# Reciprocal of the pooling counts moved into the mixer, and the last split halves of form B22 issued without a tick between them

## The chip, the cores and the metric

One core of one Trainium2 chip. The metric is device microseconds (us) of one execution. Engines: PE is TensorE (matrix products), DVE VectorE, ACT ScalarE, POOL GpSimd, SP SyncE, which here only starts transfers. A transfer is a DMA; it can also be started from the queues of ACT and POOL.

## The reference, cut to what matters

One layer over 2048 positions of 1024 channels, all in float32:

```python
xn = rmsnorm(x, norm1_g)
u_pool, zq, zf, zi, zo, zg = split(xn @ w_in)
gates = sigmoid(zg + b_gate)                       # two sets of 1024
ya = pool_mixer(u_pool, pool_w, pool_scale) @ w_pa # trailing means over 2, 4, 8, 16 positions
yb = hgrn2_mixer(zq, zf, zi, zo, ...) @ w_pb       # gated linear recurrence, 4 heads
x = x + (gates[0] * ya + gates[1] * yb) @ w_o
x = x + conv_glu_ffn(rmsnorm(x, norm2_g), w_up, conv_w, conv_b, w_down)
out = rmsnorm(x, final_g)
```

In the pooling mixer a window's sum is divided by `minimum(t, w)`, with t the position counted from 1. So only the first 15 positions of the sequence need divisors other than the window's width w.

## The kernel before, in words

**Split products.** Each float32 matrix is split into a high half (rounded to the type fp32r, a copy on ACT, line 231 for weights and line 658 for inputs) and a low half (the rest, a subtraction on DVE, lines 232 and 659). A product is three matmuls: high by high, high by low, low by high. So PE can begin a product with the high halves, and needs the low half of an input or a weight one or two matmuls later. Names ending in `h` and `l` are the halves of an input; `ops` are the split weights (both halves in one tile).

**Seven products for eight.** Positions are worked in pairs of blocks of 512, and every weight matrix in 2x2 quarters. Instead of eight block products there are seven, P1 to P7, with combined inputs. Their input forms are B11, B21 and B22 (blocks) and T1 to T4 (sums and differences): P1 takes B11, P2 B21, P3 B22, P4 T4, P5 T1, P6 T2, P7 T3. `forms_a_task` makes B11 and B21 from the first 512 rows; `forms_b_task` makes T2, T1, T3, T4 and B22, in this order, from the second 512. Each form has four parts (k = 0 to 3), each of them split. In the traces, `x_T41l` is the low half of part 1 of T4 for the input projection, `m_B223h` the high half of part 3 of B22 for the feed-forward's up-projection. Forms whose name begins with x come from the layer's input, those with m from the mixer's result. Of the sequence's two pairs of blocks, each goes through the mixer and then the feed-forward; only the first pair prepares its x forms early (`early`).

**Banks.** PE sums into banks of PSUM, eight in all. Products share banks: P6, P7 and P4 add up in one called Z, P5 and P3 in V, P1 and P2 in X. Between P7 and P4 DVE reads Z and keeps the difference as `u3` (line 1316 in the projection of recurrence input and output gate, tiles `io_u`; line 1201 in `Unit`). P4 may not write Z before that.

**Order.** Work beside PE's is written as Python generators. `mm` (line 147) counts matmuls, and every sixth calls `tick`: the weight stream converts one operand more, and each task goes on to its next `yield`. `yield n` thus waits n ticks in program order. This sets in which order instructions are issued, and each engine then works through its queue in that order, waiting at the head for what the head needs. `behind(a, b)` keeps instruction a behind b on one engine without a wait between engines. A scheduler may still move an instruction by a few places. `Stream` converts weights ahead of use: `stream.room` is how many operands ahead, `stream.low` the last low half that it made.

**Around the change.** While the first pair's `proj_io` is at P7, `setup_task` (line 601) begins. It makes masks on POOL, and, after eight transfers that add weight quarters on POOL's queue (line 165, kept in `added`), `inv`: positions 1 to 16 (line 637), the minimum with each window (line 641, four instructions), and then their reciprocals on DVE (line 643, 128x64). `inv` is read by the pooling tasks (line 942). `mixer` calls `join(setup[0])` after `proj_io`, which finishes the setup if it isn't done. In the last loop of `forms_b_task` (from line 888) the four parts of B22 are split, with one tick after each (line 903); for the m forms this runs while PE is at P4 and P3 of the feed-forward's first two units (`up_0`, `up_1`). DVE's other work there: `h` (lines 1159 and 1160, results read from banks), `e` (lines 1613 and 1616, the convolution), and `ops` (line 232).

Of the kernel before, what the change touches and what calls it, by code (L numbers as in the profile page):

```python
# [81 lines left out]
def tile_trunk(  # L82
# [16 lines left out]
    pe, act, dve, pool, sp = nc.tensor, nc.scalar, nc.vector, nc.gpsimd, nc.sync  # L99
# [43 lines left out]
    def join(task):  # L143
        while task.live:
            task.step()
# [113 lines left out]
    def behind(ins, other):  # L259

        tc.add_manual_dep(ins.ins, other.ins.name, mybir.DependencyInfo(
            mybir.DependencyClass.NoSync, mybir.DependencyReason.DATA), reason="behind")
# [17 lines left out]
    stream = Stream()  # L280
# [232 lines left out]
    def prepare():  # L513
        todo = [sums[name].make(g) for name in ("wo", "up", "dn")
                for g in range(len(sums[name].groups))]
        active = []
        while todo or active:
            while todo and len(active) < 2:
                active.append(todo.pop(0))
            g = active.pop(0)  # L520
            try:
                lag = next(g)
            except StopIteration:
                continue
            active.append(g)
            yield lag
            while quiet[0]:
                yield 1
# [63 lines left out]
    inv = const.tile([P, 4, 16], F32, tag="inv", name="inv")  # L592
# [8 lines left out]
    def setup_task():  # L601
        scratch = [hist.rearrange("p a b -> p (a b)")[:, :64], uhist.rearrange("p a b -> p (a b)")]

        def mask_of():
            scratch.reverse()
            return scratch[0]

        keys = [(h, h, 0, h) for h in (1, 2, 4, 16)]
        keys += [(8 * h + t, 2 * h, t * h, h) for h in (4, 16) for t in range(2)]
        for key, x, off, w in keys:  # L610
            nb = 64 // x
            mf = mask_of()
            behind(pool.memset(mf, 1.0), last_root[0] if len(masks) < 6 else added[3])
            v = mf.rearrange("p (b h) -> p b h", h=x)
            pool.affine_select(out=v, in_=v, pattern=[[-2 * x, nb], [0, x]],
                               compare_op=ALU.is_ge, fill=0.0, base=-off, channel_multiplier=1)
            pool.affine_select(out=v, in_=v, pattern=[[2 * x, nb], [0, x]],
                               compare_op=ALU.is_ge, fill=0.0, base=off + w - 1,
                               channel_multiplier=-1)
            m8 = const.tile([P, 64], U8, tag=f"m{key}", name=f"m{key}")  # L620
            yield 2
            pool.tensor_copy(m8, mf)
            masks[key] = m8.rearrange("p (b h) -> p b h", h=x)
        for t in range(2):
            mf = mask_of()
            behind(pool.memset(mf, 0.0), added[3])
            pool.affine_select(out=mf, in_=mf, compare_op=ALU.not_equal, fill=1.0, base=-t,
                               pattern=[[-2, 64]], channel_multiplier=1)
            m8 = const.tile([P, 64], U8, tag=f"md{t}", name=f"md{t}")
            yield 2  # L630
            pool.tensor_copy(m8, mf)
            masks[-1 - t] = m8.unsqueeze(1)
        pool.memset(hist, 0.0)
        pool.memset(uhist, 0.0)
        while len(added) < 8:
            yield 1
        ins = pool.iota(inv[:, 3], pattern=[[1, 16]], base=1, channel_multiplier=0,
                        allow_small_or_imprecise_dtypes=True)
        behind(ins, added[7])
        for g, w in enumerate(WINDOWS):  # L640
            pool.tensor_scalar(inv[:, g], inv[:, 3], float(w), None, ALU.min)
        flat_inv = inv.rearrange("p a b -> p (a b)")
        dve.reciprocal(flat_inv, flat_inv)
        for h in range(HEADS):
            pool.memset(state[h, 0], 0.0)

# [5 lines left out]
    def split(src, name, on_pool=False):  # L652
        hi = slot(name + "h", TB, F32R)
        lo = slot(name + "l", TB, F32R)
        if on_pool:
            up = pool.tensor_scalar(hi, src, 1.0, 0.0, ALU.mult, ALU.add)
        else:
            up = act.copy(hi, src)
        low = dve.tensor_tensor(lo, src, f32(hi), ALU.subtract)
        last_split[0] = up, low  # L660
        return hi, lo
# [131 lines left out]
    def forms_b_task(src, gain, forms, full, after, go, early):  # L793
# [94 lines left out]
        while len(forms["B22"]) < 4:  # L888
            k = len(forms["B22"])
            while early and len(forms.get("gate", ())) < 4:  # L890
                yield 1
            forms["B22"].append(split(b22[k], f"{name}B22{k}"))
            if early:
                behind(last_split[0][1], forms["gate"][3])
                if k < 3:
                    stream.pins[25 + k] = last_split[0]
                    while len(stream.tiles) <= 25 + k:
                        if len(stream.tiles) - N_OPS >= stream.done:
                            yield 1
                        else:  # L900
                            stream.convert()
                stream.stop = 26 + k if k < 2 else None
            yield 1
        stream.room = LOOKAHEAD

    x2d = {}
# [1 line left out]
    def forms_of(kind, b, gain, after=lambda b: lambda j: None, early=False, go=lambda: True):  # L908
        forms = {k: [] for k in ("B11", "B21", "B22", "T1", "T2", "T3", "T4", "task")}
        full = {k: [] for k in ("B11", "B21", "T2")}  # L910
        first = Task(forms_a_task((kind, b), gain, forms, full, after(b), early))
        forms["task"].append(first)
        late = Task(forms_b_task((kind, b + 1), gain, forms, full, after(b + 1), go, early))
        return forms, first, late
# [371 lines left out]
    def proj_io(b0, forms, late, vd, zd):  # L1286
# [40 lines left out]
        for p in IO_ORDER:  # L1327
            if p == "P7" and not b0:
                setup.append(Task(setup_task()))
# [38 lines left out]
    def mixer(b0, forms, late):  # L1368
# [5 lines left out]
        proj_io(b0, forms, late, vd, zd)  # L1374
        if b0 == 0:
            join(setup[0])
            prep.append(Task(prepare()))


# [440 lines left out]
    for b in range(0, SEQ // TB, 2):  # L1820
        forms, task, late = nxt
        if b:
            join(task)
        forms, task, late = mixer(b, forms, late)
        join(task)
        nxt = ffn(b, forms, late)
# [50 lines left out]
```

## Time and profile before

| | |
|---|---|
| median of 3 runs | 2542.44 us (2541.99 to 2544.25) |
| the profiled execution | 2540.99 us |
| its span, first to last instruction | 2539.3 us |
| PE busy | 2511.9 us (99%) |
| DVE busy | 1979.2 us (78%) |
| ACT busy | 1176.5 us (46%) |
| mean granted clock of PE | 0.998 of full |

A row of a timeline gives the start in us, the duration, the engine (`q` behind its name: its queue), line, operation, output and inputs, the count of merged instructions, and in brackets how long the engine was idle before it and what ended that. `PEld` are the loads of the fixed operand, which overlap the matmuls. Buffer numbers are left out of the names, so the four `io_Z` banks have one name. A matmul's row lasts longer than the step to the next one, since matmuls overlap in the array.

### The profile page before, as it was taken

The numbers are of one execution on the slowest core, as the hardware profiler recorded it, in microseconds if no ns is written. First come the engines' busy times: TensorE is split into PE (matmuls) and PEld (weight loads), VectorE is DVE, ScalarE is ACT, GpSimd is POOL, SyncE is SP. The second block draws the span as 40 slices with busy tenths as digits, with TensorE's granted clock in tenths as the row PEclk, the third lists the DMA queues.
The fourth block names the chain that finished last, engine by engine and source line by source line (L and its number), as shares of the span: only waits on it lengthen the run. The fifth ranks groups of instructions, "written<-read, shape, count | busy, mean of one in ns | idle before, by whom it ended". The sixth has DMA issues, their size and how long they took to land.

```text
span 2539.3 us, 35647 instructions
## 1 busy us (share of the span) xinstructions
PE 2511.9 (99%) x11508; PEld 2054.1 (81%) x11508; DVE 1979.2 (78%) x3508; ACT 1176.5 (46%) x2218; POOL 752.6 (30%) x1127
## 2 busy tenths in 40 slices
PE   9999999999999999999999999999999999999998
PEld 7788887788788888888888888888887888888886
DVE  7799778498999777885586778765979888778755
ACT  6434434334545444554554343442355544445534
POOL 4334343002344334461230212200033432325410
PEclk9999999999999999999999999999999999999999
DMA  8787777767898889997444343447443454447952
GB/s 274 241 200 220 201 212 227 228 214 242 209 246 240 221 233 242 264 364 243 133 146 150 107 135 109 137 150 224 149 154 110 153 154 136 150 137 236 327 165 97
DMA packets 252331, 493.75 MB, mean 194 GB/s; under 512 B 26544, under 2 KB 43056, under 8 KB 251824
## 3 DMA queue, kind: packets, MB, share of 16 engines
q1 hardware_dynamic: 184512, 313.60, 39.1%
q0 software_dynamic: 42656, 112.74, 17.6%
q10 hardware_dynamic: 24976, 65.13, 7.5%
q8 instruction: 91, 1.49, 0.3%
q14 instruction: 96, 0.79, 0.1%
HBM read 381.79 MB, written 187.17 MB: 224 GB/s over the span
## 4 chain that ended last, share of the span: by engine, by line
PE 90%; DVE 6%; issue 1%; DMA 1%; ACT 1%; POOL 0%; SPq 0%; DVEq 0%; POOLq 0%; ACTq 0%
PE dn_P L148 16%; PE up_Z L148 14%; PE up_X L148 10%; PE up_V L148 9%; PE wo_P L148 6%; PE gr_Z L148 4%; PE pb L148 4%; PE pa L148 3%; PE gr_X L148 3%; PE gr_V L148 3%; PE fr_Z L148 2%; PE io_Z L148 2%; PE fr_X L148 2%; PE fr_V L148 2%; PE io_V L148 1%
## 5 line engine op out<-in xcount | busy, mean ns | idle before, releaser
L231 ACT CAST ops<-raw 128x512 fp32r<-128x512 f32 x744 | 459.7, 620 | 823.1 <-PE dn_P L148 180.5
L232 DVE TENSOR_TENSOR ops<-raw,ops 128x512 fp32r<-128x512 f32 x744 | 554.5, 749 | 218.3 <-ACT ops L231 210.3
L1613 DVE SCALAR_TENSOR_TENSOR e<-h,cols,e 128x512 f32<-128x512 f32 x176 | 143.6, 819 | 31.2 <-ACT e L1611 24.2
L1611 ACT ACTIVATE e<-h,cols 128x512 f32<-128x512 f32 x176 | 142.6, 814 | 25.6 <-DVE h L1160 18.9
L1616 DVE SCALAR_TENSOR_TENSOR e<-h,cols,e 128x512 f32<-128x512 f32 x176 | 134.0, 770 | 2.7
L962 POOL DMA_DIRECT2D g_P<-dg_P x154 | 84.0, 547 | 159.7 <-PE dn_P L148 113.3
L1270 POOL TENSOR_TENSOR gf_P<-e,e 128x512 f32<-128x512 f32 x44 | 62.2, 1415 | 149.6 <-DVE e L1622 93.0
L1270 POOL TENSOR_TENSOR gf_P<-gf_P,e 128x512 f32<-128x512 f32 x44 | 59.0, 1341 | 72.1 <-DVE e L1622 71.6
L1606 POOL COPY h<-h 128x2 f32<-128x2 f32 x88 | 40.9, 476 | 125.0 <-DVE h L1159 118.2
L1408 POOL TENSOR_TENSOR q<-q,qs 128x512 f32<-128x512 f32 x16 | 21.7, 1358 | 187.4 <-ACT qs L1407 180.8
L1445 ACT ACTIVATE gt<-gt,cols 128x512 f32<-128x512 f32 x48 | 34.8, 725 | 85.9 <-DVE gt L1160 61.3
L1620 ACT ACTIVATE e<-e 128x512 f32<-128x512 f32 x88 | 55.6, 631 | 39.8 <-DVE e L1616 39.4
L1608 POOL COPY hist<-h 128x2 f32<-128x2 f32 x88 | 37.8, 429 | 116.6 <-DVE h L1160 114.8
L1160 DVE TENSOR_TENSOR h<-up_u,up_V 128x512 f32<-128x512 f32 x88 | 60.1, 683 | 11.3 <-PE up_V L148 10.8
L1245 DVE TENSOR_TENSOR x<-x,wo_P 128x512 f32<-128x512 f32 x88 | 56.1, 683 | 12.0 <-PE wo_P L148 11.8
L1245 DVE TENSOR_TENSOR ac<-ac,dn_P 128x512 f32<-128x512 f32 x72 | 47.1, 682 | 16.8 <-PE dn_P L148 16.6
L1012 POOL COPY qm<-q 128x64 f32<-128x64 f32 x64 | 27.1, 452 | 99.0 <-issue 26.2
L1027 PE MATMUL pl<-qm,k 128*128 128x192 f32 x256 | 50.6, 327 | 3.7 <-DVE k L1048 3.6
L1636 POOL DMA_DIRECT2D dg_P<-gf_P x88 | 50.8, 577 | 8.3 <-POOL gf_P L1270 7.4
L1195 ACT COPY up_e<-up_X 128x512 f32<-128x512 f32 x44 | 25.8, 586 | 57.8 <-PE up_X L148 52.7
L1606 POOL COPY h<-hist 128x2 f32<-128x2 f32 x88 | 46.0, 530 | 20.6 <-issue 20.6
L1027 PEld LDWEIGHTS pl<-qm,k 128*128 128x128 f32 x256 | 43.9, 189 | 9.6 <-POOL u L926 2.3
(1285 smaller groups left out, 8088.4 us busy)
## 6 DMA issues: line engine op xcount, KB each, us to landing
g_P<-dg_P POOLq DMA_DIRECT2D x154, 256.0 KB, 6.0
raw<-in_w_up_t SPq DMA_DIRECT2D x132, 256.0 KB, 3.2
raw<-in_w_in_t SPq DMA_DIRECT2D x98, 256.0 KB, 3.3
dg_P<-gf_P POOLq DMA_DIRECT2D x88, 256.0 KB, 4.0
dg_P<-e SPq DMA_DIRECT2D x66, 256.0 KB, 3.8
raw<-in_w_dn SPq DMA_DIRECT2D x66, 256.0 KB, 3.7
x<-in_x SPq DMA_DIRECT2D x64, 256.0 KB, 4.9
gd<-gt ACTq DMA_DIRECT2D x64, 256.0 KB, 3.1
```

The costliest lines, as they stand in the source:

```text
L148: count[1] = pe.matmul(*args, **kw)
L231: self.mark = act.copy(hi, v)
L232: low = self.low = dve.tensor_tensor(lo, v, f32(hi), ALU.subtract)
L962: eng.dma_start(t, d)
L1027: ins = pe.matmul(pa_[:, c * 192 : c * 192 + 192], ks[:, (i + c) * P : (i + c + 1) * P], mv[:, c].rearrange("p s x -> p (s x)"), start=Tru ...
L1160: return dve.tensor_tensor(dst, t, ps, ALU.add if how == "add" else ALU.subtract)
L1245: dve.tensor_tensor(t, t, ps[j], ALU.add if sg > 0 else ALU.subtract)
L1270: pin(eng.tensor_tensor(t, x0, x1, op))
L1606: pool.tensor_copy(h[:, 0:2], hist[:, mt] if hf == 0 else hs[s, 0][:, TB : TB + 2])
L1611: in_turn(act.activation(t, h[:, 2:], AF.Identity, bias=col(o_cb + mt), scale=col(o_cw + 4 * MF + mt)))
L1613: in_turn(second(dve.scalar_tensor_tensor(t, h[:, 1 : 1 + TB], col(o_cw + 2 * MF + mt), t, ALU.mult, ALU.add)))
L1616: dve.scalar_tensor_tensor(t, h[:, 0:TB], col(o_cw + mt), t, ALU.mult, ALU.add)
```

## The change

The reciprocal leaves `setup_task` and is issued in `mixer` after the setup is joined, behind the stream's last low half. In the last loop of `forms_b_task` the tick after each part of B22 stays for the x forms and goes for the m forms, so that their four parts are issued in one go.

```diff
@@ setup_task
         for g, w in enumerate(WINDOWS):
             pool.tensor_scalar(inv[:, g], inv[:, 3], float(w), None, ALU.min)
-        flat_inv = inv.rearrange("p a b -> p (a b)")
-        dve.reciprocal(flat_inv, flat_inv)
         for h in range(HEADS):
             pool.memset(state[h, 0], 0.0)
@@ forms_b_task, last loop
                 stream.stop = 26 + k if k < 2 else None
-            yield 1
+            if src[0] != "m":
+                yield 1
         stream.room = LOOKAHEAD
@@ mixer
         if b0 == 0:
             join(setup[0])
+            flat_inv = inv.rearrange("p a b -> p (a b)")
+            behind(dve.reciprocal(flat_inv, flat_inv), stream.low)
             prep.append(Task(prepare()))
```

**The reciprocal on DVE.** In DVE's queue before, at P7 of the first `proj_io`, it stands between the first and the second of the four `io_u`:

```order
L865 TENSOR_TENSOR x_t_924<-x_b_364,x_t_563 128x512
L1316 TENSOR_TENSOR io_u_0_967<-io_Z_701,io_e_0_459 128x512
L643 RECIPROCAL inv<-inv 128x64
L1316 TENSOR_TENSOR io_u_1_977<-io_Z_702,io_e_1_469 128x512
L1316 TENSOR_TENSOR io_u_2_982<-io_Z_703,io_e_2_474 128x512
L1316 TENSOR_TENSOR io_u_3_987<-io_Z_704,io_e_3_479 128x512
L659 TENSOR_TENSOR x_T41l<-x_t_924,x_T41h 128x512
```

With the change it stands some 35 instructions further on, at the end of `proj_io`, behind a weight's low half for the first unit (`v` is a result of P3; the lines are those of the changed kernel):

```order
L1159 TENSOR_TENSOR v_1_3_1272<-io_u_3_779,io_V_788 128x512
L232 TENSOR_TENSOR ops_1253<-w31s_1250,ops_1253 128x512
L1377 RECIPROCAL inv<-inv 128x64
L232 TENSOR_TENSOR ops_1284<-raw_1018,ops_1284 128x512
L232 TENSOR_TENSOR ops_1307<-raw_1007,ops_1307 128x512
```

The four `io_u` now follow each other, and nothing else changes its place on DVE between the two positions.

**The low halves on DVE.** At P4 and P3 of the feed-forward's first units DVE's queue before was:

```order
L659 TENSOR_TENSOR m_B220l<-m_b_6612,m_B220h 128x512
L232 TENSOR_TENSOR ops_7028<-raw_6817,ops_7028 128x512
L659 TENSOR_TENSOR m_B221l<-m_b_6641,m_B221h 128x512
L1159 TENSOR_TENSOR h_0_1_0_6972<-up_0_Z,up_0_e_6548 128x512
L1613 SCALAR_TENSOR_TENSOR e_0_0_0_6975<-h_0_0_0_6716,cols,e_0_0_0_6975 128x512
L659 TENSOR_TENSOR m_B222l<-m_b_6676,m_B222h 128x512
L232 TENSOR_TENSOR ops_7043<-raw_6845,ops_7043 128x512
L1616 SCALAR_TENSOR_TENSOR e_0_0_0_6975<-h_0_0_0_6716,cols,e_0_0_0_6975 128x512
L659 TENSOR_TENSOR m_B223l<-m_b_6704,m_B223h 128x512
L1159 TENSOR_TENSOR h_1_1_0_7004<-up_1_Z,up_1_e_6568 128x512
```

and with the change it is:

```order
L657 TENSOR_TENSOR m_B220l<-m_b_6612,m_B220h 128x512
L232 TENSOR_TENSOR ops_7022<-raw_6817,ops_7022 128x512
L657 TENSOR_TENSOR m_B221l<-m_b_6641,m_B221h 128x512
L657 TENSOR_TENSOR m_B222l<-m_b_6676,m_B222h 128x512
L657 TENSOR_TENSOR m_B223l<-m_b_6704,m_B223h 128x512
L1158 TENSOR_TENSOR h_0_1_0_6985<-up_0_Z,up_0_e_6548 128x512
L1158 TENSOR_TENSOR h_1_1_0_7009<-up_1_Z,up_1_e_6568 128x512
L232 TENSOR_TENSOR ops_7043<-raw_6845,ops_7043 128x512
```

Part 2 has moved ahead of one `h` and one `e`, part 3 ahead of these, a weight and a second `e`. The same happens in the second pair's feed-forward.

**The high halves on ACT**, same place; before:

```order
L658 CAST m_B220h<-m_b_6612 128x512
L231 CAST ops_7028<-raw_6817 128x512
L658 CAST m_B221h<-m_b_6641 128x512
L1611 ACTIVATE e_0_0_0_6975<-h_0_0_0_6716,cols 128x512
L658 CAST m_B222h<-m_b_6676 128x512
L231 CAST ops_7043<-raw_6845 128x512
L307 DMA su3s_6097<-su3s_6096 16x16384
L658 CAST m_B223h<-m_b_6704 128x512
```

and with the change:

```order
L656 CAST m_B220h<-m_b_6612 128x512
L231 CAST ops_7022<-raw_6817 128x512
L656 CAST m_B221h<-m_b_6641 128x512
L656 CAST m_B222h<-m_b_6676 128x512
L656 CAST m_B223h<-m_b_6704 128x512
L231 CAST ops_7043<-raw_6845 128x512
```

Parts 2 and 3 now follow part 1 directly; the first `e` and the weight `ops_7043` come behind them. Further on, ACT's first Silu of `e` (line 1620, with the load of its table) has moved behind one weight and one `e` more.

## The prediction

> **What bounds the kernel now.** I read the page first, its busy shares and the chain that ended last, then the waits of PE, then the timelines around the longest of them.
>
> ```profile
> PE 2511.9 (99%) x11508; PEld 2054.1 (81%) x11508; DVE 1979.2 (78%) x3508; ACT 1176.5 (46%) x2218; POOL 752.6 (30%) x1127
> ...
> PE 90%; DVE 6%; issue 1%; DMA 1%; ACT 1%; POOL 0%; SPq 0%; DVEq 0%; POOLq 0%; ACTq 0%
> ```
>
> PE is busy for 99% of the span and is nine tenths of the chain, and the change takes no matmul away. So it can only win time in which PE stands still or runs slowly. The waits of PE (engine, line, releaser: us in total, times, longest) name two that the change touches:
>
> ```profile
> PE pl L1027 <- DVE k L1048: 3.6, 2, 1.9
> PE io_Z L148 <- DVE io_u L1316: 3.0, 1, 3.0
> ...
> PE up_V L148 <- DVE m_B223l L659: 1.8, 2, 0.9
> ```
>
> **First wait: io_Z for io_u.** The chain that ended last (start, us, what) shows what stands behind it:
>
> ```profile
> 70.88 3.84 DMA raw<-kw2ioP
> ...
> 75.28 0.35 POOL raw L165
> ...
> 78.28 0.26 POOL inv L641
> ...
> 78.56 0.04 DVE inv L643
> ...
> 79.71 12.26 PE io_Z L148 x45
> ```
>
> A weight's transfer lands, POOL can issue its addition, then POOL makes `inv`, then DVE inverts it, and only then comes the second `io_u`, for which PE waits. The pooling counts have nothing to do with `io_u`; the reciprocal merely stands ahead of it in DVE's queue. The timeline of this place:
>
> ```profile
> 74.64 0.69 DVE L1316 TENSOR_TENSOR io_u<-io_Z,io_e 128x512 f32<-128x512 f32 x1 [2.60 <-PE io_Z L148]
> ...
> 75.60 0.40 PE L148 MATMUL io_Z<-ops,x_T33l 128*128 128x512 f32 x1
> ...
> 75.84 0.63 PE L148 MATMUL io_Z<-ops,x_T40h 128*128 128x512 f32 x2
> 76.31 0.40 PE L148 MATMUL io_Z<-ops,x_T40l 128*128 128x512 f32 x1
> ...
> 78.56 0.55 DVE L643 RECIPROCAL inv<-inv 128x64 f32<-128x64 f32 x1 [3.23 <-POOL inv L641]
> 79.03 1.82 DVE L1316 TENSOR_TENSOR io_u<-io_Z,io_e 128x512 f32<-128x512 f32 x3
> ...
> 79.71 1.22 PE L148 MATMUL io_Z<-ops,x_T40h 128*128 128x512 f32 x2 [3.01 <-DVE io_u L1316]
> ...
> 80.77 0.68 DVE L659 TENSOR_TENSOR x_T41l<-x_t,x_T41h 128x512 fp32r<-128x512 f32 x1
> ...
> 81.97 0.68 DVE L232 TENSOR_TENSOR ops<-raw,ops 128x512 fp32r<-128x512 f32 x1
> ...
> 91.81 2.03 PE L148 MATMUL io_V<-ops,x_B220h 128*128 128x512 f32 x8
> ...
> 102.96 0.39 PE L148 MATMUL fr_X<-x_f0h,ops 128*128 128x512 f32 x1
> ```
>
> P4 and P3 of this stage are 48 matmuls each (4 parts, 4 banks, 3 products). P3 takes 102.96 - 91.81 = 11.15 us, 0.232 us a step. P4 takes 91.81 - 75.84 = 15.97 us. So this place loses 4.82 us, more than the 3.0 of the waits. A plain gap is 79.71 - (76.31 + 0.23) = 3.17 us; for the other 1.65 look at the windows, whose third number from the right is PE's granted clock:
>
> ```profile
> 76.50:79.70 3.20, 0.20 (x1) 0.00 (x0) 1.14 (x3) 0.00 (x0) 1.73 (x6) 1.00 0.91 136
> 79.70:83.50 3.80, 3.79 (x10) 3.06 (x11) 3.71 (x7) 1.14 (x2) 0.00 (x0) 0.55 0.16 28
> 83.50:91.80 8.30, 8.30 (x37) 6.74 (x36) 8.16 (x12) 7.65 (x14) 2.57 (x2) 1.00 0.77 233
> ```
>
> After the gap the clock is 0.55 for 3.8 us: 3.8 x 0.45 = 1.7 us, which is the rest.
>
> **Second wait: the low halves of B22**, once in each feed-forward:
>
> ```profile
> 682.97 0.40 PE L148 MATMUL up_V<-m_B223h,ops 128*128 128x512 f32 x1
> ...
> 684.24 0.50 PE L148 MATMUL up_V<-m_B223l,ops 128*128 128x512 f32 x1 [0.87 <-DVE m_B223l L659]
> 684.57 0.40 PE L148 MATMUL up_V<-m_B223h,ops 128*128 128x512 f32 x1
> ...
> 1933.97 0.39 PE L148 MATMUL up_V<-m_B223h,ops 128*128 128x512 f32 x1
> ...
> 1935.58 0.40 PE L148 MATMUL up_V<-m_B223h,ops 128*128 128x512 f32 x1
> ```
>
> Two steps of 0.23 take 684.57 - 682.97 = 1.60 us, so 1.14 us are lost; the second time 1.61, so 1.15. DVE and ACT at the first of the two:
>
> ```profile
> 679.77 0.69 DVE L659 TENSOR_TENSOR m_B221l<-m_b,m_B221h 128x512 fp32r<-128x512 f32 x1
> 680.37 0.69 DVE L1159 TENSOR_TENSOR h<-up_Z,up_e 128x512 f32<-128x512 f32 x1
> ...
> 683.50 0.69 DVE L659 TENSOR_TENSOR m_B223l<-m_b,m_B223h 128x512 fp32r<-128x512 f32 x1
> ...
> 679.18 0.81 ACT L1611 ACTIVATE e<-h,cols 128x512 f32<-128x512 f32 x1
> ```
>
> Between parts 1 and 3 DVE does an `h`, two `e`, a weight and part 2; an `e` stands between parts 1 and 2 on ACT.
>
> **The change part by part.**
>
> *Reciprocal away from P7.* DVE starts `x_T41l` and the low half of `ops` 1.20 us apart, with one more between, so 0.60 us is the step of a DVE instruction of 512. The second `io_u` starts at 74.64 + 0.60 = 75.24 instead of 79.03, the third at 75.84. The fourth waits for PE's last P7 matmul, 75.60 + 0.40 = 76.00, and ends at about 77.1. PE wants the second bank at 76.54, the third at 77.2, the fourth at 78.6: all three are in time, and 4.82 us go, the gap and the slow clock.
>
> What is late next? DVE goes on with `x_T41l` (77.05), a difference for T4 (77.65) and the low half of the next weight (78.25 to 78.95). In PE's queue, P4's seventeenth matmul is the first to read that low half, at 75.84 + 16 x 0.232 = 79.55. That is 0.6 us to spare, little, but enough. From there DVE is full up to P3:
>
> ```profile
> 88.98 1.79 DVE L659 TENSOR_TENSOR x_B220l<-x_b,x_B220h 128x512 fp32r<-128x512 f32 x1
> ...
> 93.67 1.10 PE L148 MATMUL io_V<-ops,x_B220l 128*128 128x512 f32 x4
> ```
>
> Before, this half ended at 90.77, 2.9 us before its use at 93.67. DVE comes 79.03 - 75.24 = 3.79 us earlier, PE 4.82, so 1.9 us remain. The transfers that fill P3's weights are issued by POOL as before, from 75.28 on, and the windows show DMA at 0.16 after 79.7: they have landed before ACT asks for them at about 82.
>
> *Reciprocal put back.* One instruction of 0.55 us in DVE's queue behind the last weight of `proj_io`, where its input is 20 us old. Its readers are the pooling tasks, the first of them at 181.5 (the count row of line 942; times are the shortest, middle and longest in ns, then first and last start in us):
>
> ```profile
> L942 DVE TENSOR_TENSOR p<-s,inv x4: 174/184/1011, 181.5 to 372.4; 128x16 f32<-128x16 f32 x4
> ```
>
> It costs DVE 0.55 us in a stretch in which DVE has over 9 us free, the first of these windows:
>
> ```profile
> 103.00:120.00 17.00, 17.00 (x75) 13.82 (x74) 7.68 (x12) 5.86 (x9) 3.58 (x3) 1.00 0.90 312
> 150.00:165.00 15.00, 13.09 (x63) 10.87 (x62) 14.43 (x45) 3.58 (x7) 6.23 (x9) 1.00 0.93 232
> ```
>
> The weight behind it is for P2 of the first unit, which PE begins four products of 12 matmuls, 11 us, after `fr_X` at 102.96: nothing lost. Without that cover it would cost 0.55.
>
> *B22 in one go.* Behind `m_B221l` (679.77), part 2 starts at 680.37 and part 3 at 680.97 and ends at 681.66, in place of 684.19. PE wants part 3 at 682.97 + 0.23 = 683.20: 1.5 us to spare. Their high halves follow at 679.18 and 679.7 on ACT, in the place of the first `e`, and are done by 680.3. So both stalls go: 1.14 + 1.15 = 2.29 us. What is put back are `h`, `e` and one weight, by 1.2 to 3 us. No matmul reads `h` or `e` before the down-projection. The weight `ops_7043` is read five products of 12 matmuls after P3 begins, 14 us later. The earlier return to four operands ahead changes only when ACT converts; I cost it at nothing.
>
> **Sum.** 4.82 + 2.29 = 7.11 us. The profiled execution has 2540.99 us (2539.3 span and 1.7 around it), so it would have 2533.9. It lies 1.45 below the median of the runs, 2542.44, which becomes **2535.3**, 0.28% less.
>
> **Rivals.**
>
> *The slow clock belongs to this one execution.* [...] As a mechanism of this kernel: if the timed runs mostly lack the stretch that the windows show, only 3.17 + 2.29 = 5.46 us go, and the median becomes 2537.0. For it: the gap is the only one over 2 us in PE's waits, so no second case shows that the clock always falls. Against it: the profiled execution has the stretch and is yet faster than all timed runs. Chance 0.12.
>
> *The recurrence takes it back.* In the stretch from 150 to 165 DVE is busy for 14.43 of 15 us, and there PE waits for `k` (line 1048), 1.9 us. If that chain does not start earlier, PE arrives 4.8 us sooner and waits that much longer: only B22's 2.29 remain, 2540.1. Against it: DVE's rows before, from 103 to 120, are mostly idle and wait for PE's results, so the chain starts with PE and moves along. Chance 0.14, with anything between the two.
>
> *It doesn't do what it says.* Another instruction takes the reciprocal's place, or ACT's high halves come late, and B22's stall stays: 2542.44 - 4.82 = 2537.6. Against it, every instruction between has a row above with time to spare. Chance 0.05.
>
> *Slower: the first Silu of each feed-forward.* ACT now has it and its table load behind one weight and one `e` more, and DVE's queue holds `up_u` of unit 3 behind a convolution that waits for ACT behind them. PE's P7 of that unit may not write the bank before:
>
> ```profile
> 693.51 0.68 DVE L1197 TENSOR_TENSOR up_u<-up_e,up_Z 128x512 f32<-128x512 f32 x1
> ...
> 701.46 0.40 PE L148 MATMUL up_Z<-m_T30h,ops 128*128 128x512 f32 x1
> ```
>
> There are 701.46 - 694.19 = 7.3 us to spare. What has moved ahead is one `e` (0.81 above) and one weight, which waits for PE's end of a product; with that wait I estimate 3 us. Were it 15, PE would lose 7.7 us twice, and the median would be 2542.44 - 7.11 + 15.4 = 2550.7; it is slower than before from 7.3 + 7.11/2 = 10.8 us on. Chance 0.03.
>
> **How the numbers follow.** The forecast has 0.66 and its own range is 2533.5 to 2537; the rivals have 0.12, 0.14, 0.05 and 0.03. 0.2% is 5.1 us, about what a measurement of this kernel can tell from no change; the line is at 2537.4. Faster by more: the forecast and half of the clock's rival, 0.72. Slower by more: the Silu, 0.03. Within: the rest, 0.25. The range goes from 2533.5, 1.8 below the forecast for waits that shrink with the shift, up to 2540.0, next to the recurrence's case.
>
> **What would show it.** Right: no wait of PE for `io_u`, P4 of the first projection in 11.2 us at clock 1.00; none for `m_B223l`; the pairs of `up_V` rows 0.46 us apart; the wait for `k` still about 1.9. Wrong: a new wait of PE for `ops` or `x_T41l` near 79, for `x_B22` parts near 88, or a longer one for `k` near 155.

## The result, and the profile after

The changed kernel takes **2533.76 us** (median of 6 runs, 2532.39 to 2536.34) against 2542.9 (6 runs, 2541.99 to 2544.25) beside it: ratio 0.9964, 95% interval 0.9951 to 0.9977, so 9.1 us less, with 5.8 to 12.5 in the interval. The forecast was 2535.3 and 7.1 us less. The profiled execution has 2532.39 us and a span of 2530.7, where the sum had 2533.9. Line numbers differ a little between kernels, since each has lines more or less; in the changed one `io_u` is 1315, the halves of inputs 656 and 657, the reciprocal 1377.

The page of the changed kernel, its busy shares and the shares of the chain that ended last:

```profile
PE 2509.1 (99%) x11508; PEld 2053.6 (81%) x11508; DVE 1978.5 (78%) x3508; ACT 1176.1 (46%) x2218; POOL 753.4 (30%) x1127
...
PE 91%; DVE 5%; issue 1%; DMA 1%; POOL 1%; ACT 1%; SPq 0%; DVEq 0%; POOLq 0%; ACTq 0%
```

PE is busy for 2.8 us less, with as many matmuls: those of the slow stretch count as busy and took longer (before, 8 in the 3.40 us from 79.70 on at clock 0.50, then 22 in 4.90 us at 1.00), and the stretch's 1.65 us are the larger part of it. Its waits (engine, line, releaser: us in total, times, longest):

```profile
PE x_t L722 <- DVE x_xs L716: 3.7, 5, 1.2
PE pl L1026 <- DVE k L1047: 3.5, 2, 1.8
PE pt L1144 <- DVE ot L1138: 1.8, 1, 1.8
PE warm L682 <- POOL ident L563: 1.4, 1, 1.4
PE ur_Z L148 <- DVE ur_u L1196: 1.1, 1, 1.1
```

Both waits that the change aimed at are gone, for `io_u` (3.0 before) and for `m_B223l` (1.8). Of the smaller ones a `gr_u` of 1.0 is missing too. The wait for `k` is as long as before. The windows of the first projection's P4 (length, busy time of PE, PEld, DVE, ACT and POOL, then PE's granted clock, DMA's share, GB/s), over the same times as before:

```profile
76.50:79.70 3.20, 3.20 (x16) 2.58 (x15) 3.11 (x6) 1.14 (x2) 2.46 (x4) 1.00 0.45 86
79.70:83.50 3.80, 3.80 (x18) 3.10 (x17) 3.66 (x7) 3.22 (x7) 1.82 (x4) 1.00 0.91 190
```

Where PE stood still for 3.00 of 3.20 us and then ran at clock 0.55 for 3.8, it now is busy throughout at 1.00. The timeline there:

```profile
74.52 2.48 DVE L1315 TENSOR_TENSOR io_u<-io_Z,io_e 128x512 f32<-128x512 f32 x4 [1.86 <-PE io_Z L148]
...
75.72 0.63 PE L148 MATMUL io_Z<-ops,x_T40h 128*128 128x512 f32 x2
...
78.13 0.68 DVE L232 TENSOR_TENSOR ops<-raw,ops 128x512 fp32r<-128x512 f32 x1
...
85.14 0.68 DVE L657 TENSOR_TENSOR x_B220l<-x_b,x_B220h 128x512 fp32r<-128x512 f32 x1
...
86.85 2.03 PE L148 MATMUL io_V<-ops,x_B220h 128*128 128x512 f32 x8
...
88.72 1.10 PE L148 MATMUL io_V<-ops,x_B220l 128*128 128x512 f32 x4
```

The four `io_u` run in one go, and P4 takes 86.85 - 75.72 = 11.13 us, where 11.2 was forecast and 15.97 measured before: 4.84 us. B22 in DVE's queue, and PE's steps beside it, in the first feed-forward:

```profile
673.49 0.69 DVE L657 TENSOR_TENSOR m_B221l<-m_b,m_B221h 128x512 fp32r<-128x512 f32 x1
674.09 0.69 DVE L657 TENSOR_TENSOR m_B222l<-m_b,m_B222h 128x512 fp32r<-128x512 f32 x1
674.70 0.68 DVE L657 TENSOR_TENSOR m_B223l<-m_b,m_B223h 128x512 fp32r<-128x512 f32 x1
...
676.66 0.39 PE L148 MATMUL up_V<-m_B223h,ops 128*128 128x512 f32 x1
676.89 0.40 PE L148 MATMUL up_V<-m_B223l,ops 128*128 128x512 f32 x1
677.13 0.39 PE L148 MATMUL up_V<-m_B223h,ops 128*128 128x512 f32 x1
```

The low half of part 3 ends at 675.38 and is wanted at 676.89, 1.5 us later, as forecast; the pair of `m_B223h` stands 0.47 us apart, where it was 1.60.

### The profile page after: what moved, and what is told of

It is laid out like the page before. It is cut to its first block, busy times and chain, and to the rows that moved or that the text cites. A ratio compares the mean times of both kernels' runs of the same rounds, so it can differ in the third digit from the quotient of the medians.

```text
span 2530.7 us, 35649 instructions
## 1 busy us (share of the span) xinstructions
PE 2509.1 (99%) x11508; PEld 2053.6 (81%) x11508; DVE 1978.5 (78%) x3508; ACT 1176.1 (46%) x2218; POOL 753.4 (30%) x1127
## 4 chain that ended last, share of the span: by engine, by line
PE 91%; DVE 5%; issue 1%; DMA 1%; POOL 1%; ACT 1%; SPq 0%; DVEq 0%; POOLq 0%; ACTq 0%
PE dn_P L148 16%; PE up_Z L148 14%; PE up_X L148 10%; PE up_V L148 10%; PE wo_P L148 6%; PE gr_Z L148 4%; PE pb L148 4%; PE pa L148 3%; PE io_Z L148 3%; PE gr_X L148 3%; PE fr_Z L148 2%; PE gr_V L148 2%; PE io_V L148 2%; PE fr_X L148 2%; PE fr_V L148 2%; PE pl L1026 1%
```

## The experiments

The theory is the sum of the prediction: DVE's wait for POOL's `inv` costs the gap and a slow clock behind it, and the ticks cost B22's two stalls. Against it stood that the slow clock was an accident of one execution, that the reciprocal's place or its own 0.55 us costs, and, since 2 us more came than the sum has, that one of the two parts carries something beyond its term.

### The reciprocal alone

```diff
@@ forms_b_task, against the change
-            if src[0] != "m":
-                yield 1
+            yield 1
```

> The reciprocal moved, the tick after each part of B22 kept. The change took 9.1 us off the median (2542.9 to 2533.76) where the prediction's sum was 7.1, so 2 us more have to be placed. Theory A (three pieces that add up, as predicted; the rest is small waits that shift): this kernel saves 4.8 us against before, 2538.1, and PE's two waits for m_B223l stay at 0.9 us each. Rival B (the 2 us more belong to the B22 part): also 4.8. Rival C (the gap ahead of io_u is longer in most executions than in the one profiled, since it ends when a weight's transfer has landed and POOL has made inv): 6 to 7 us, 2536.5.

Measured: 2537.36 us (11 runs, 2534.75 to 2540.16) against 2542.59 (21 runs): ratio 0.998, interval 0.9971 to 0.9989. That is 5.2 us for a term of 4.82. B22's two stalls are back in its waits of PE, beside longer ones for `gr_u`:

```profile
PE gr_Z L148 <- DVE gr_u L1195: 3.2, 2, 2.0
...
PE up_V L148 <- DVE m_B223l L657: 1.7, 2, 0.9
```

Every engine issues the same instructions in the same order as in the changed kernel until B22 is split, near 670 us. Yet ahead of that this profile is 3.5 us later than the changed kernel's. So the `gr_u` waits belong to the execution, not to the ticks.

### B22 alone

```diff
@@ forms_b_task, against the kernel before
-            yield 1
+            if src[0] != "m":
+                yield 1
```

> The ticks of B22 taken away, the reciprocal where it was before. Theory A: 2.3 us less than before, 2540.6; PE's waits for m_B223l are gone, the wait for io_u is there with a slow clock behind it. Rival B: 4 us or more less. Rival C: 2.3 us, and a wait for io_u that differs from the 3.0 us of before's trace, since its end depends on when the transfer lands. If the slow clock belongs to one execution alone, the clock after the gap is 1.00 here.

Measured: 2540.09 us (11 runs, 2536.71 to 2542.83) against 2542.59: ratio 0.999, interval 0.9981 to 0.9999. That is 2.5 us for a term of 2.29, and no wait for `m_B223l`. The two parts alone make 5.2 + 2.5 = 7.7 us. In its trace the gap for `io_u` is there again and longer than in the profile of before, and again a slow stretch follows. Its windows:

```profile
76.60:80.30 3.70, 0.10 (x1) 0.00 (x0) 1.12 (x3) 0.00 (x0) 2.25 (x7) 1.00 0.73 104
80.30:81.20 0.90, 0.87 (x3) 0.73 (x4) 0.90 (x2) 0.00 (x0) 0.00 (x0) 0.89 0.83 148
81.20:84.50 3.30, 3.30 (x9) 2.58 (x8) 3.22 (x6) 1.14 (x2) 0.00 (x0) 0.51 0.12 9
```

PE resumes at 80.33, has a few steps of the usual length, and is then at clock 0.51 for 3.3 us, in which every matmul takes 0.43 us instead of 0.23.

### The reciprocal behind the second, and behind the third io_u

The diff is that of the first of the two kernels; the other has `u3s[2]`.

```diff
@@ setup_task, against the change; u3s collects the io_u of the stage
+        flat_inv = inv.rearrange("p a b -> p (a b)")
+        behind(dve.reciprocal(flat_inv, flat_inv), u3s[1])
@@ mixer
-            flat_inv = inv.rearrange("p a b -> p (a b)")
-            behind(dve.reciprocal(flat_inv, flat_inv), stream.low)
```

> The changed kernel, with the reciprocal behind the second io_u. PE has three matmuls more before it must wait, so the gap is 3 x 0.23 = 0.7 us shorter than with the reciprocal behind the first: about 2.5 us if inv is ready at 78.5. If every gap of this kind is followed by a slow stretch, the clock is about 0.55 for some 4 us after it and P4 takes 11.15 + 2.5 + 1.7 = 15.3 us. If the clock falls only after about 3 us of standing still, it stays 1.00 and P4 takes 13.6 us.

> The changed kernel, with the reciprocal behind the third io_u. PE has three matmuls more of P4's first part and three of its second before it must wait: a gap of about 1.1 us if inv is ready at 78.5, more if it is late. By a threshold of about 3 us the clock stays 1.00 and P4 takes 12.3 us; if every gap brings the slow stretch, 14 us.

Measured, one run each: 2541.72 us behind the second, 2538.55 behind the third. DVE's wait does not shrink, since POOL is no earlier: the reciprocals start at 80.67 and 80.06, after idle times of 3.94 and 3.06 us. The expectations had `inv` ready at 78.5, and so their gaps of 2.5 and 1.1 us are missed: P4 takes 16.60 us instead of 15.3, and 14.22 instead of 12.3. What changes is how many banks PE can fill in the meantime. Windows of the two kernels, the second one and then the third:

```profile
78.10:81.80 3.70, 0.10 (x1) 0.00 (x0) 1.13 (x3) 0.00 (x0) 2.24 (x7) 1.00 0.75 112
81.80:83.10 1.30, 1.28 (x5) 1.05 (x6) 1.30 (x3) 0.00 (x0) 0.00 (x0) 0.98 0.46 82
83.10:86.50 3.40, 3.40 (x9) 2.67 (x8) 3.17 (x6) 2.01 (x4) 0.00 (x0) 0.50 0.30 78
```

```profile
79.20:81.20 2.00, 0.07 (x1) 0.00 (x0) 1.15 (x3) 0.00 (x0) 0.68 (x3) 1.00 1.01 163
81.20:83.00 1.80, 1.20 (x4) 0.67 (x4) 1.75 (x3) 0.62 (x2) 0.00 (x0) 1.00 0.33 57
```

Behind the second, a gap of 3.7 us and again a stretch of 3.4 us at half clock; so this kernel did not try a gap under 3 us, as it was meant to. Behind the third, a gap of 2.0 us and clock 1.00 behind it. The threshold of about 3 us in the two expectations was the author's supposition: no run shows it, and elsewhere the clock fell behind waits of 1.8 and 2.0 us too (last section). In the kernel with the reciprocal behind the third P4 also meets the wait that the prediction named as next in line, the low half of the weight behind the late `io_u`; the timeline of that kernel:

```profile
81.21 0.74 PE L148 MATMUL io_Z<-ops,x_T40h 128*128 128x512 f32 x2 [1.94 <-DVE io_u L1319]
...
83.01 0.50 PE L148 MATMUL io_Z<-ops,x_T41h 128*128 128x512 f32 x1 [0.60 <-DVE ops L232]
```

### One tick fewer, and twice the ticks

```diff
@@ forms_b_task, against the change: the first kernel
-            if src[0] != "m":
+            if src[0] != "m" or k < 2:
                 yield 1
@@ the second kernel
-            if src[0] != "m":
-                yield 1
+            yield 2 if src[0] == "m" else 1
```

> The change, but of the ticks of the m forms only those after part 2 and part 3 go; the one after part 0 and the one after part 1 stay. In DVE's queue one h, two e and one weight then stand among parts 2 and 3 again, as before. If only the place in DVE's queue matters: the two stalls for m_B223l are back, 0.9 us each in the waits and 1.1 us each in the steps, no wait for io_u, and a time 2.3 us over that of the change, about 2536. If it is the number of ticks that matters: half of the stalls, 2535. The first 670 us issue the same instructions in the same order as the change on every engine, so what differs there in the small waits (gr_u, k, at) is the difference between two executions; I expect up to 3 us in all.

Measured in one run: 2537.19 us, and `m_B223l` has its two waits of 0.9 again. Among the four parts there is one tick fewer than in the kernel before, yet DVE's queue holds the same there, two others between parts 1 and 2 and two between parts 2 and 3. The number of ticks does not decide; what stands in DVE's queue among the parts does.

> The change with two ticks after each part of the m forms where the kernel before has one. Part 3 then stands ten places behind part 0 in DVE's queue, against eight before and four in the change. If DVE's place sets the stall: at 0.62 us a place part 2 comes 2.4 us late and part 3 hardly later than that, so PE loses about 2.4 us in each feed-forward against 1.14 before and 0 in the change: 4.8 us over the change, about 2538.6. If DVE has slack that catches up: no more than the stall of before, 2536.

Measured: 2539.12 us (11 runs, 2536.76 to 2542.06), ratio 0.9985, interval 0.9976 to 0.9994, against 2533.04 of the change on the same chip: 6.1 us given back, 4.8 expected. Its timeline, DVE's rows and then PE's:

```profile
676.29 0.68 DVE L657 TENSOR_TENSOR m_B221l<-m_b,m_B221h 128x512 fp32r<-128x512 f32 x1
676.89 0.68 DVE L1157 TENSOR_TENSOR h<-up_Z,up_e 128x512 f32<-128x512 f32 x1
677.50 0.74 DVE L1616 SCALAR_TENSOR_TENSOR e<-h,cols,e 128x512 f32<-128x512 f32 x1
678.16 0.68 DVE L232 TENSOR_TENSOR ops<-raw,ops 128x512 fp32r<-128x512 f32 x1
678.76 0.74 DVE L1613 SCALAR_TENSOR_TENSOR e<-h,cols,e 128x512 f32<-128x512 f32 x1
679.42 0.68 DVE L657 TENSOR_TENSOR m_B222l<-m_b,m_B222h 128x512 fp32r<-128x512 f32 x1
...
678.24 0.50 PE L148 MATMUL up_V<-m_B222h,ops 128*128 128x512 f32 x1 [0.48 <-ACT m_B222h L656]
680.16 0.50 PE L148 MATMUL up_V<-m_B222l,ops 128*128 128x512 f32 x1 [1.42 <-DVE m_B222l L657]
680.49 0.39 PE L148 MATMUL up_V<-m_B222h,ops 128*128 128x512 f32 x1
```

DVE is not idle for a moment here; four instructions between parts 1 and 2 make the low half of part 2 late. PE waits first for its high half, from ACT (0.48 us), and then for the low half (1.42 us), which ends the stall. By the starts of the matmuls, set against those of the change, PE loses 2.50 us here and 2.49 in the second feed-forward, where the places in DVE's queue gave 2.4. Part 3's low half follows part 2's directly and costs nothing more.

### The reciprocal in its old place, its input earlier

```diff
@@ setup_task, against the change
-        while len(added) < 8:
+        while len(added) < 6:
             yield 1
...
-        behind(ins, added[7])
+        behind(ins, added[5])
...
+        while len(added) < 8:
+            yield 1
+        flat_inv = inv.rearrange("p a b -> p (a b)")
+        while not u3s:
+            yield 1
+        behind(dve.reciprocal(flat_inv, flat_inv), u3s[0])
@@ mixer
-            flat_inv = inv.rearrange("p a b -> p (a b)")
-            behind(dve.reciprocal(flat_inv, flat_inv), stream.low)
```

> The change with the reciprocal back in its old place, between the first and the second io_u in DVE's queue; instead POOL makes its input two weight transfers earlier, behind the sixth and not the eighth. If the loss was DVE's wait for POOL: the input is ready near 73 us, the reciprocal costs 0.6 us of DVE, the second io_u ends at about 76.5 against 76.54, the low half of the weight at 79.5 against 79.5, so nothing over 0.3 us is lost, and the time is that of the change, 9 us under the kernel before. If the reciprocal's place itself costs: a wait of PE for io_u or ops of 1 us or more at 76 to 80, and 2 us or more of the gain gone.

Measured: **2533.6 us** (5 runs, 2531.43 to 2535.81) against 2542.97 (15 runs): ratio 0.9965, interval 0.9952 to 0.9977, the same as the change. Its timeline:

```profile
71.15 2.11 POOL L643 TENSOR_SCALAR inv<-inv 128x16 f32<-128x16 f32 x4
...
74.69 0.69 DVE L1323 TENSOR_TENSOR io_u<-io_Z,io_e 128x512 f32<-128x512 f32 x1 [1.85 <-PE io_Z L148]
...
75.30 0.54 DVE L649 RECIPROCAL inv<-inv 128x64 f32<-128x64 f32 x1
...
75.75 1.82 DVE L1323 TENSOR_TENSOR io_u<-io_Z,io_e 128x512 f32<-128x512 f32 x3
...
76.59 0.62 PE L148 MATMUL io_Z<-ops,x_T40h 128*128 128x512 f32 x2
```

With its input ready at 73.26 the reciprocal starts as soon as DVE is free, between the first and the second `io_u` as before, and PE has no gap: the second bank's matmul stands where it should, 0.24 us behind the first bank's last. So neither the reciprocal's place nor its 0.54 us cost anything; its wait for POOL did, and moving POOL's five instructions for `inv` up by two weight transfers is worth as much as moving the reciprocal.

### The change once more

> The changed kernel once more, as it is, on the chip that runs the other kernels of this call. 9 us under the kernel before. If the 1.5 to 2 us beyond the named terms belong to the change, its profile has the small waits of the first one (gr_u 0.4, k 3.5, at none). If they belong to single executions, gr_u, k and at differ by 1 to 3 us again, as they do between the change and the reciprocal alone, which issue the same up to 670 us.

Measured: 2533.04 us (5 runs, 2532.01 to 2539.77) against 2542.97: ratio 0.9966, interval 0.9953 to 0.9978. Its waits of PE have a `gr_u` that the first profile of the change lacks, and less of `k`:

```profile
PE pl L1026 <- DVE k L1047: 1.5, 1, 1.5
PE pl L1026 <- POOL u L925: 1.5, 1, 1.5
...
PE gr_Z L148 <- DVE gr_u L1196: 1.3, 2, 1.1
```

## Why the prediction was right, and what its size missed

**The reciprocal's wait, 4.82 us.** Right in mechanism and size. P4 went from 15.97 to 11.13 us; by the starts of the same matmuls in both traces 4.85 us are gained between 72 and 100 us. That the wait and not the instruction costs was argued in the prediction and is shown by the kernel with the earlier input.

**What is late next.** Right: nothing. The low half of the weight ends at 78.81 and is read at 79.45, 0.6 us to spare as forecast; the kernel with the reciprocal behind the third `io_u` delays it and PE waits 0.60 us for it. `x_B220l` has 88.72 - 85.82 = 2.9 us to spare, 1.0 more than forecast, because its row is 0.68 us long and not 1.79. The step that put POOL's transfers "as before, from 75.28 on" failed: in the change POOL issues them at 77.15, and `inv` is ready only at 81.73, 3.2 us later than before. No weight came late, and with the reciprocal gone from there nothing waits for `inv`; it is inverted at 99.9 and first read at 176.3.

**B22, 1.14 + 1.15 us.** Right in mechanism: both waits gone, and with the order of before they return in each kernel that has it. By the starts of the matmuls the two places gave 1.17 and 1.21 us.

**The slow clock as an accident (chance 0.12).** Wrong as put: of three traces with a gap over 3 us (3.17, 3.79 and 3.79 between the end of a step and the next matmul) all three have the slow stretch, and it cost 8 matmuls x 0.2 us, about 1.6, each time. But a part of it stands: behind the same wait of 1.8 us the clock fell in one execution and not in another (last section), and that moves single executions.

**The recurrence takes it back (0.14).** It did not. The wait for `k` at 154.02 is 1.77 us against 1.9, and DVE's chain came forward with PE, as the row against this rival had it.

**Slower by the first Silu (0.03).** It did not come about. Rows of the changed kernel, `up_u` of unit 3 and the matmul that needs its bank:

```profile
686.80 0.68 DVE L1196 TENSOR_TENSOR up_u<-up_e,up_Z 128x512 f32<-128x512 f32 x1
...
694.02 0.40 PE L148 MATMUL up_Z<-m_T30h,ops 128*128 128x512 f32 x1
```

6.5 us to spare of 7.3; what moved ahead of it cost 0.7 us (before, it ended at 694.19, which is 686.7 in times of the changed kernel), where 3 were estimated.

**The size.** 9.1 us came where the sum had 7.1; in the two later comparisons 9.9 (the change again) and 9.4 (the earlier input). That 2533.76 lies in the forecast's own range, 2533.5 to 2537, is in part luck: the same kernel run again took 2533.04. The term that is short is B22's; the rest can't be given to the change by these runs. This table has the start of the same matmul in each kernel's trace less that in the first trace of the change, in us, at times of the latter:

```
                        72     100    660    700    1260   1300   1900   1940   end
before                  0.12   4.97   6.28   7.45   7.25   6.44   6.95   8.16   8.57
B22 alone               0.12   5.60   8.18   8.20   8.20   7.62   7.60   7.60   7.60
reciprocal alone        0.44   0.44   3.51   4.66   4.47   3.99   4.48   5.73   6.16
one tick fewer          0.04   0.04   2.17   3.33   3.14   2.66   3.14   4.35   4.77
earlier input           0.17   0.18   1.09   1.12   1.12   1.17   1.14   1.14   1.14
the change once more    0.21   0.21   0.90   0.93   0.93   0.97   0.95   0.95   0.95
```

Three things are to be read from it. *B22:* from 660 to 1260 and from 1300 to the end the three kernels with the old order lose 3.1 us (before: 0.97 + 2.13; reciprocal alone: 0.96 + 2.17; one tick fewer: 0.97 + 2.10), the three others, with the new order, nothing. The stalls are 2.4 of it (660 to 700, and 1900 to 1940). Another 0.7 is the sum of differences of under 0.03 us in single steps of the matmuls, 0.2 less from 700 to 1260 and 0.9 more behind 1300, the same in all three; the prediction's "I cost it at nothing" for what moves around B22 missed them, and what makes them stays open. *The gap:* 5.5 us in the trace of B22 alone against 4.85 in that of before, since POOL was later. *The rest:* between 1260 and 1300 the first four kernels gain 0.5 to 0.8 us on the change, at the second pair's transpositions, where PE waits 0.8 us for `x_xs` in the trace of the change and 0.3 in that of before; neither term has this, and its cause stays open. And between 100 and 660 these kernels differ by up to 3.1 us, though the reciprocal alone, one tick fewer and the change once more issue the same there as the change itself, instruction by instruction; the two that differ most of these, the reciprocal alone and one tick fewer, have a slow stretch there (at 390 and 467). So 4.8 to 5.5 and 3.1, together 7.9 to 8.6 us, are the change's by mechanism; the half to 2 us beyond, and the 0.5 to 0.8 that the transpositions may take back, are within the scatter of such small waits and within the interval, and these runs can't resolve them.

## What to carry to other kernels

Before a wait of the busiest engine is priced, look at what its releaser itself waits for: here an instruction of 0.55 us that nobody needed for another 100 us stood at the head of a queue and held three others, and either moving it or feeding it earlier brought the same. In an engine's queue without idle time count the places between the parts of an operand: here each was worth 0.6 us, and the ticks put four of them between parts 1 and 3, 2.4 us against a slack of 1.5. And where a trace shows slow matmuls behind a gap, price them with the gap: 1.65 us beside 3.17 here.

## What the runs showed of the hardware

**PE's clock behind a wait.** In six places windows of these traces show a lower granted clock behind a wait of PE, 0.50 to 0.58. In the trace of before it is 0.50 from 79.70 to 83.10, directly behind the gap, and 1.00 from there on; in those of B22 alone and of the reciprocal behind the second `io_u` it falls 0.7 and 1.2 us after PE resumed, an estimate from the clocks of 0.89 and 0.98 in the windows above. The waits ahead of the six were 3.0 us for `io_u` (before), 3.6 for `io_u` (B22 alone, and behind the second `io_u`), 2.0 for `gr_u` (the reciprocal alone) and 1.8 for `ot` (B22 alone, and one tick fewer).

Behind other waits of 1.8 to 1.94 us the clock stayed at 1.00: 1.9 us for `k` and 1.8 for `ot` in the trace of before, 1.94 for `io_u` behind the third, 1.8 for `ot` in the change once more. All ten traces have the wait of 1.8 us for `ot` (line 1138 in the change). Windows there, of the kernel with one tick fewer and of the change once more:

```profile
464.90:466.90 2.00, 0.36 (x2) 0.00 (x0) 1.41 (x3) 1.66 (x3) 0.00 (x0) 1.00 1.06 274
466.90:470.40 3.50, 3.30 (x9) 2.61 (x10) 2.71 (x7) 0.00 (x0) 0.00 (x0) 0.57 1.11 269
470.40:474.00 3.60, 3.60 (x17) 2.92 (x17) 0.69 (x1) 0.46 (x1) 0.00 (x0) 0.94 1.06 358
```

```profile
464.00:466.20 2.20, 1.54 (x7) 0.94 (x5) 0.43 (x1) 1.08 (x3) 0.00 (x0) 1.00 1.07 253
466.20:470.00 3.80, 2.62 (x12) 2.17 (x13) 3.69 (x9) 0.64 (x2) 0.00 (x0) 1.00 1.11 274
```

In the first the clocks of 0.57 and 0.94 behind the wait make 3.50 x 0.43 + 3.60 x 0.06 = 1.7 us lost, by estimate; in the second nothing was lost beyond the wait. So the length of a wait does not tell in these traces whether slow matmuls follow; what does is not shown by them, and no run set out to try it. It is one source of the scatter between executions.

**The minima of `inv` on POOL took 252 ns before and 540 with the change.** The four of them in the two traces (times are the shortest, middle and longest in ns):

```profile
L641 POOL TENSOR_SCALAR inv<-inv x4: 245/252/281, 77.3 to 78.3; 128x16 f32<-128x16 f32 x4
```

```profile
L641 POOL TENSOR_SCALAR inv<-inv x4: 524/540/754, 79.2 to 81.0; 128x16 f32<-128x16 f32 x4
```

Before, DVE stood idle for 3.23 us until they were done; with the change DVE was busy beside them, for 3.66 of the 3.80 us from 79.70 on. In the three other kernels in which DVE waits for `inv` the four took 1.23 us together, 1.24 before; with the earlier input, where DVE works until 72.84 of their 71.15 to 73.26, 2.11 us, 478 ns in the middle. That DVE's work is the cause was not tried by itself.
